# Keys of branch B: the copy in the other half of the partitions made by a DMA, not from PSUM

## The chip, the cores and the metric

The kernel runs on one core of a Trainium2 chip. The metric is device time in microseconds (us) of one execution, as the median of several. Its engines: TensorE (PE in the profile, with its weight loads as PEld), VectorE (DVE), ScalarE (ACT), GpSimd (POOL) and SyncE (SP). DMAs are issued by SP and ACT, each with a hardware queue of its own, called q1 and q10 in the profile.

## The reference

One layer of an encoder with two token mixers in parallel, applied to two inputs apart, a prompt of 1024 tokens and a sample of 512, all in float32, with D_MODEL = 1024:

```
xn = RMSNorm(x)
z  = xn @ W_in            # q_A k_A v_A | q_B k_B v_B | gate_A gate_B
o_A = grouped-query attention, normalised and rotated q/k, 8 heads of 64
o_B = 2-D neighbourhood attention, 8 heads of 64: the tokens are a grid 64 wide;
      each query sees a window of min(8, rows) x 16 tokens, with a learned bias
      by the 2-D offset
mix = (sigmoid(gate_A) * (o_A @ W_pA) + sigmoid(gate_B) * (o_B @ W_pB)) @ W_out
x = x + mix;  x = x + relu(RMSNorm(x) @ W_up)^2 @ W_down;  final RMSNorm
```

The change is in branch B, in how its keys are laid down for the scores `q @ k`.

## The kernel before

**Precision.** A float32 value is kept as two float32r numbers, a high part (a rounded copy) and a low part (the value less its high part). A product of two such values takes three matmuls, high by high, high by low and low by high: the helper `mm3`, whose three matmuls are lines 191, 192 and 193. Splitting costs an ACT copy for the high part and a DVE subtraction for the low part.

**Stages.** The two trunks run one after the other, the sample first, through the function `run`; then the MLP for all tokens. Within `run`, branch B (phase phB) is a stage of its own: from about 181 to 345 us of the span for the sample (T = 512, NB = 1 block of 512 tokens), from about 770 to 1050 us for the prompt (T = 1024, NB = 2).

**Branch B.** Heads go in four pairs (pr = 0 to 3). `qkproj` projects a pair's queries and keys for each block tb of 512 tokens. Each of the two takes 24 matmuls (8 slices of the model dimension, three matmuls each) into one bank of PSUM, tiles `pqbs` and `pkbs`, and is then split into SBUF. The scores of a head contract over 128 partitions where a head has only 64 dimensions: the queries' tile `qBs` has the high part in one half of the partitions and the low part in the other, and the keys' tile `kBs` (one per head, e = 0 or 1) has the same key values in both halves, with the high parts in its plane 0 and the low parts in plane 1. Two matmuls (line 949) then give all the products of parts. Head e of a pair comes out of the projection in the 64 partitions from 64e on, so one half of `kBs` is in place and the other is a copy into the other partitions. Before, both are made from PSUM: two ACT copies (line 909) and two DVE subtractions (line 911) for each head, each of 64 partitions x 512, and eight operations for a block. There are 4 + 8 = 12 blocks, so each of the two lines runs 48 times. The subtractions of either half read the high part of the half that is in place.

The unit of the attention is a head and one or two of the four column strips: `s_unit` makes the scores `sbs` (line 949), the masked and negated scores with their minimum (`sbss`, `msbs`, line 951 on DVE), the exponential `pbs` on ACT (955) and the scaling on POOL (959); `t_unit` transposes the probabilities by TensorE into `ptbs` (974 for the sample, 980 for the prompt) and splits them into `bhs` on ACT (983) and DVE (984); `v_unit` multiplies by the values `vss` into `obs` (1006) and adds the halves up into `os_Bs` (1011 on ACT, 1013 on DVE, 1026 on POOL), which ACT stores (1028, or for the last pair's heads into `oXs`).

**What fills the gaps.** The loop over units (from line 1054 on) runs three units at different stages at once, with the projection of the next pair (`qkproj` is a generator that is advanced eight steps at a time) and with "fill": the projections of gate_B (`gpss`, weights `w_gs`, tanh into `sgs` at line 430, stored as `zgs` by an ACT DMA at 431), and toward the end the projection `ppas` of branch A's output `oXs`, split by line 180 on ACT and 186 on DVE as the weights are.

**What sets the order.** The code gives a program order; the framework then schedules the instructions of all engines by a model of their costs and writes a fixed sequence for each engine. An engine works through its sequence in order. A change to some operations therefore moves others too, on all engines. DMAs that ACT issues stand in ACT's sequence: the issue waits, there, until its data are ready. PSUM has four banks for tiles of 512 columns, shared by `pqbs`, `pkbs`, `gpss`, `ptbs`, `obs` and `ppas`.

Of the kernel before, what the change touches and what calls it, by code (L numbers as in the profile page):

```python
# [11 lines left out]
F32 = mybir.dt.float32  # L12
# [49 lines left out]
def encoder(ctx: ExitStack, tc: tile.TileContext, xs, outs, w):  # L62
    nc = tc.nc
# [23 lines left out]
    def slot(shape, dt, name, left=False):  # L87
        return (s8l if left else s8r).tile(shape, dt, tag="s8", name=name)
# [4 lines left out]
    def mm(name):  # L93
        return pmm.tile([P, 512], F32, tag="mm", name=name)

    def big(name):
        return pbig.tile([P, 1024], F32, tag="big", name=name)
# [92 lines left out]
    def mm3(out, ah, al, bh, bl, start, stop, **kw):  # L190
        nc.tensor.matmul(out, ah, bh, start=start, stop=False, **kw)  # L191
        nc.tensor.matmul(out, ah, bl, start=False, stop=False, **kw)  # L192
        nc.tensor.matmul(out, al, bh, start=False, stop=stop, **kw)  # L193
# [159 lines left out]
    class Trunk:  # L353
# [37 lines left out]
        def xh(self, tb, c):  # L391
            return self.xhl[tb][0][c // 4][:, c % 4, :]

        def xl(self, tb, c):
            return self.xhl[tb][1][c // 4][:, c % 4, :]

    def run(tr, nxt, first):
        N, x, T, NT, NB = tr.N, tr.x, tr.T, tr.NT, tr.NB
# [85 lines left out]
        for g in range(2):  # L484
            with phase(f"phR{N}_{g}") as ph:
# [74 lines left out]
                kT = slot([P, 2, T], F32R, f"kT{N}_{g}")  # L560
# [47 lines left out]
                for tt in range(NT):  # L608
                    tb, j = divmod(tt, 4)
# [233 lines left out]
        with phase(f"phB{N}") as ph:  # L843
# [24 lines left out]
            def qkproj(pr, wqk, dest):  # L868
                wq, wk = wqk
                qT = slot([P, 2, T], F32R, f"qB{N}_{pr}")  # L870
                kT = [slot([P, 2, T], F32R, f"kB{N}_{pr}_{e}") for e in range(2)]
                dest[pr] = (qT, kT)
                for tb in range(NB):
                    cs = slice(tb * 512, tb * 512 + 512)
                    pq = mm(f"pqb{N}_{pr}_{tb}")
                    for k in range(NC8):
                        mm3(pq, wq[k][0], wq[k][1], xh(tb, k), xl(tb, k), k == 0, k == NC8 - 1)
                        yield
                    for e in range(2):
                        hs = slice(64 * e, 64 * e + 64)  # L880
                        ls = slice(64 - 64 * e, 128 - 64 * e)

                        src = pq[hs].rearrange("p (r j c) -> p j r c", j=4, c=16)

                        def strip_view(s_):
                            return qT[s_, e, :].rearrange("p (j r c) -> p j r c", j=4, c=16)[
                                :, :, tb * 8 : tb * 8 + 8, :
                            ]

                        dst_h, dst_l = strip_view(hs), strip_view(ls)  # L890
                        nc.scalar.activation(dst_h, src, AF.Copy, scale=0.125)
                        for jj in range(4):
                            nc.vector.scalar_tensor_tensor(
                                dst_l[:, jj],
                                src[:, jj],
                                0.125,
                                dst_h[:, jj].bitcast(F32),
                                op0=ALU.mult,
                                op1=ALU.subtract,
                            )  # L900
                    pk = mm(f"pkb{N}_{pr}_{tb}")
                    for k in range(NC8):
                        mm3(pk, wk[k][0], wk[k][1], xh(tb, k), xl(tb, k), k == 0, k == NC8 - 1)
                        yield
                    for e in range(2):
                        hs = slice(64 * e, 64 * e + 64)
                        ls = slice(64 - 64 * e, 128 - 64 * e)
                        for os_ in (hs, ls):
                            nc.scalar.activation(kT[e][os_, 0, cs], pk[hs], AF.Copy)
                        for os_ in (hs, ls):  # L910
                            nc.vector.tensor_tensor(
                                kT[e][os_, 1, cs], pk[hs], kT[e][hs, 0, cs].bitcast(F32), op=ALU.subtract
                            )

            qk = {}
# [129 lines left out]
            for _ in qkproj(0, wqk, qk):  # L1045
                pass
# [7 lines left out]
            for i in range(n + LS + LV):  # L1054
# [4 lines left out]
                if i < n:  # L1059
                    s_unit(units[i])  # L1060
                    if units[i][1][0] == 1 and units[i][0] + 1 < 8:
                        prep(units[i][0] + 1)
                    if i % per == (6 if JN == 1 else 2) and i + 2 < n:
                        while held:
                            held.pop(0)()
                        qp = qkproj(i // per + 1, wqk, qk)
                        for _ in range(NC8):
                            next(qp)
                    if i % per == per - 1 and qp is not None:
                        for _ in qp:  # L1070
                            pass
                        qp = None
# [23 lines left out]
        with phase(f"phG{N}") as ph:  # L1096
# [69 lines left out]
            for half in range(2):  # L1166
                wo = wos[half]
                hc = slice(half * 512, half * 512 + 512)
                for tt in range(NT):
                    tb, j = divmod(tt, 4)  # L1170
# [23 lines left out]
                    if half == 0 and NB == 1:  # L1194
                        if tt == 0:
                            both = [big(f"op{N}_{i}") for i in range(2)]
# [36 lines left out]
                    if half == 1:  # L1233
# [5 lines left out]
                        if nxt is None:  # L1239
# [10 lines left out]
                            if 3 <= tt <= 5:  # L1250
# [6 lines left out]
                                both = [big(f"pt0_{j}_{i}") for i in range(2)]  # L1257
# [618 lines left out]
```

## Time and profile before

| | us |
|---|---|
| median of 3 runs | 2132.78 |
| the runs | 2132.7, 2132.78, 2134.22 |
| the profiled execution | 2134.04 |
| its span | 2132.2 |
| sample's branch B, 181 to 345 us | 164.0 |
| prompt's branch B, 770 to 1050 us | 280.0 |

The profile shows one execution. Its span is the time from the first to the last instruction on the core. How its rows are read: a row of the timeline has the start in us, the duration in us, the engine, the line, the operation, output <- inputs by the tiles' names without their numbers, the shape, the number of operations that the row holds, and in brackets how long the engine stood idle before and what released it. A row of waits has the engine, the tile and line that waited, after "<-" what it waited for, then the total in us, the number of times and the longest. A row of windows has start and end, the length, then for each engine the busy time and the number of operations in brackets, TensorE's granted clock (1.00 is full speed), the busy share of the DMA engines and GB/s. A row of a line has how often it ran and the shortest, median and longest duration in ns.

### The profile page before, as it was taken

The page shows a single profiled execution, that of the slowest core. Times are in us where ns is not written, and L with a number is a line of the kernel's source. Part 1 is how long each engine was busy: PE and PEld are TensorE (multiplying, and loading weights), DVE is VectorE, ACT ScalarE, POOL GpSimd, SP SyncE. Part 2 cuts the span into 40 slices and gives each one's busy share as a digit, 9 for nine tenths or more (in the row PEclk, how much of TensorE's full clock was granted, in tenths as well). Part 3 has the DMA queues.
Part 4 walks back from the last instruction along what each step waited for, and adds up shares of the span by engine and source line. Part 5 has one row for each costly group of instructions (what it writes and reads, how often), then busy time and mean ns, then how long its engine had stood idle before and what let it go on. Part 6 is the DMA issues. An engine that isn't in the chain of part 4 may idle for free. (4 is left out here: it accounts for less than half of the span.)

```text
span 2132.2 us, 31826 instructions
## 1 busy us (share of the span) xinstructions
PE 2114.7 (99%) x10982; PEld 1849.5 (87%) x10982; DVE 1473.7 (69%) x2805; ACT 1114.3 (52%) x2345; POOL 388.2 (18%) x506
## 2 busy tenths in 40 slices
PE   9999999999999999999999999999999999999998
PEld 8888788988898888888888999999999988888887
DVE  6675686777667754656782977778777777759563
ACT  5654664556536644655531566566655643434352
POOL 2232420433233223433300200003000000000000
PEclk9999999999999999999999999999999999999999
DMA  6435567620221132433472666578445799688561
GB/s 187 130 105 171 156 187 242 195 72 30 62 83 53 43 108 85 123 106 108 138 247 101 212 200 193 161 249 210 158 145 159 255 351 341 220 275 281 172 197 70
DMA packets 319578, 350.91 MB, mean 165 GB/s; under 512 B 31160, under 2 KB 255032, under 8 KB 319417
## 3 DMA queue, kind: packets, MB, share of 16 engines
q1 hardware_dynamic: 278071, 279.91, 41.8%
q10 hardware_dynamic: 35666, 51.93, 7.0%
q0 software_dynamic: 5680, 17.04, 2.8%
q8 instruction: 87, 1.43, 0.3%
q14 instruction: 74, 0.61, 0.1%
HBM read 264.85 MB, written 87.88 MB: 165 GB/s over the span
## 5 line engine op out<-in xcount | busy, mean ns | idle before, releaser
L193 PE MATMUL dn<-wd,al 128*128 128x512 f32 (+1 forms) x624 | 242.4, 389 | 0.0
L192 PE MATMUL dn<-wd,ah 128*128 128x512 f32 (+1 forms) x624 | 242.4, 388 | 0.0
L191 PE MATMUL dn<-wd,ah 128*128 128x512 f32 (+1 forms) x624 | 242.4, 388 | 0.0
L1289 ACT ACTIVATE ah<-ar 128x512 fp32r<-128x512 f32 x168 | 104.4, 627 | 203.9 <-PE dn L192 183.3
L1290 DVE TENSOR_TENSOR al<-ar,ah 128x512 fp32r<-128x512 f32 x168 | 115.3, 693 | 77.5 <-ACT ah L1289 65.0
L193 PEld LDWEIGHTS dn<-wd,al 128*128 128x128 f32 x624 | 117.2, 188 | 24.2
L192 PEld LDWEIGHTS dn<-wd,ah 128*128 128x128 f32 x624 | 117.2, 188 | 24.1
L191 PEld LDWEIGHTS dn<-wd,ah 128*128 128x128 f32 x624 | 117.2, 188 | 24.0
L735 POOL TENSOR_SCALAR ps<-ps,rls 128x1024 f32<-128x1024 f32 (+1 forms) x96 | 96.8, 1010 | 215.7 <-DVE rls L734 201.3
L775 DVE TENSOR_TENSOR ptls<-pTs,pths 128x512 fp32r<-128x512 f32 x160 | 107.6, 686 | 37.8 <-ACT pths L774 37.1
L774 ACT ACTIVATE pths<-pTs 128x512 fp32r<-128x512 f32 x160 | 94.1, 598 | 73.7 <-PE pTs L769 71.7
L729 DVE TENSOR_REDUCE nms<-ss 128x1 f32<-128x1024 f32 (+1 forms) x96 | 99.8, 1041 | 24.9 <-PE ss L727 24.4
L176 POOL TENSOR_TENSOR rs_f<-ms_f,mhalf 128x1 f32<-128x1 f32 x6 | 4.0, 666 | 590.7 <-DVE ms_f L172 590.7
L732 ACT ACTIVATE ps<-ss,nms 128x1024 f32<-128x1024 f32 (+1 forms) x96 | 93.2, 972 | 23.8 <-DVE nms L729 19.8
L191 PE MATMUL gpss<-xs_0h,w_gs 128*128 128x512 f32 x256 | 104.7, 409 | 0.3 <-ACT w_gs L180 0.2
L769 PEld LDWEIGHTS pTs<-ident,ps 128*128 128x128 f32 x640 | 78.1, 140 | 28.2 <-POOL ps L735 4.1
L193 PE MATMUL gpss<-xs_0h,w_gs 128*128 128x512 f32 x256 | 101.0, 394 | 0.0
L192 PE MATMUL gpss<-xs_0l,w_gs 128*128 128x512 f32 x256 | 100.8, 394 | 0.0
L769 PE MATMUL pTs<-ident,ps 128*128 128x128 f32 x640 | 98.9, 274 | 1.2 <-DVE ptls L775 0.5
L1289 ACT ACTIVATE A<-S 128x512 fp32r<-128x512 f32 x128 | 76.0, 624 | 30.0 <-DVE S L1352 26.8
L1408 ACT ACTIVATE c<-c 128x384 f32<-128x384 f32 x97 | 50.8, 524 | 69.0 <-DVE c L1407 69.0
L1290 DVE TENSOR_TENSOR A<-S,A 128x512 fp32r<-128x512 f32 x128 | 84.4, 685 | 3.4 <-ACT A L1289 3.4
(344 smaller groups left out, 6402.3 us busy)
## 6 DMA issues: line engine op xcount, KB each, us to landing
ar<-ud SPq DMA_DIRECT2D x120, 512.0 KB
br<-in_w_mlp_down_dram SPq DMA_DIRECT2D x72, 512.0 KB
rawu<-in_w_mlp_up_dram SPq DMA_DIRECT2D x64, 512.0 KB
ud<-c ACTq DMA_DIRECT2D x128, 192.0 KB
raw_gs<-in_w_in_dram SPq DMA_DIRECT2D x32, 512.0 KB
zgs<-sgs ACTq DMA_DIRECT2D x48, 256.0 KB
ud<-cs SPq DMA_DIRECT2D x64, 192.0 KB
raw_os<-in_w_out_dram SPq DMA_DIRECT2D x16, 512.0 KB
```

What stands on the lines that cost most here:

```text
L191: nc.tensor.matmul(out, ah, bh, start=start, stop=False, **kw)
L192: nc.tensor.matmul(out, ah, bl, start=False, stop=False, **kw)
L193: nc.tensor.matmul(out, al, bh, start=False, stop=stop, **kw)
L729: nc.vector.tensor_reduce(nm_, s, axis=AX.X, op=ALU.max, negate=True)
L732: nc.scalar.activation(p, s, AF.Exp, bias=nm_, accum_out=l)
L735: nc.gpsimd.tensor_scalar(p, p, rl, 1.0, op0=ALU.mult, op1=ALU.mult)
L769: nc.tensor.transpose(pt[:, j * P : (j + 1) * P], PP[u, j][:, kc * P : (kc + 1) * P], ident)
L774: nc.scalar.activation(hi, pt, AF.Copy)
L775: nc.vector.tensor_tensor(lo, pt, hi.bitcast(F32), op=ALU.subtract)
L1289: nc.scalar.activation(hi, src, AF.Copy)
L1290: nc.vector.tensor_tensor(lo, src, hi.bitcast(F32), op=ALU.subtract)
L1408: nc.scalar.activation(t, t, AF.Relu)
```

## The change

```
-                    for e in range(2):
-                        hs = slice(64 * e, 64 * e + 64)
-                        ls = slice(64 - 64 * e, 128 - 64 * e)
-                        for os_ in (hs, ls):
+                    both = (slice(0, 64), slice(64, 128))
+                    by_dma = pr > 0 or tb + 1 < NB
+                    for e, hs in enumerate(both):
+                        for os_ in (hs,) if by_dma else (hs, both[1 - e]):
                             nc.scalar.activation(kT[e][os_, 0, cs], pk[hs], AF.Copy)
-                        for os_ in (hs, ls):
+                    for e, hs in enumerate(both):
+                        for os_ in (hs,) if by_dma else (hs, both[1 - e]):
                             nc.vector.tensor_tensor(
                                 kT[e][os_, 1, cs], pk[hs], kT[e][hs, 0, cs].bitcast(F32), op=ALU.subtract
                             )
+                    for e, hs in enumerate(both):
+                        if by_dma:
+                            nc.scalar.dma_start(
+                                kT[e][both[1 - e], :, cs].bitcast(F32), kT[e][hs, :, cs].bitcast(F32)
+                            )
```

In 10 of the 12 blocks only the half that is in place is made from PSUM, by one ACT copy and one subtraction for each head. ACT then issues a DMA for each head, which copies high and low part of that half into the other half of the partitions, 256 KB. Two blocks stay as they were: those whose scores follow the first projection, the sample's pair 0 and the second block of the prompt's pair 0. For all twelve, the code now gives both heads' ACT copies, then both heads' subtractions, where it gave one head after the other. In the changed file ACT's copies keep line 909, the subtractions become line 912, the DMAs are line 917, and the lines behind grow by 6 (949 becomes 955, 983 becomes 989, 1006 becomes 1012).

The order of all engines moves with it, inside the two stretches of branch B only. Two places, both at the last pair of the prompt, second block (pair 3; heads 6 and 7; `kBs_3_0` and `kBs_3_1` are the keys of its two heads, the last number of a name is a running number). First ACT's sequence before:

```order
L909 ACTIVATE kBs_3_0_10994<-pkbs_3_1_11146 64x512 x2
L180 ACTIVATE oXs_0_3_11227<-rawos_0_3_11225 128x1024
L983 ACTIVATE bhs_5_0_11188<-ptbs_5_0_0_11189 128x3x128
L983 ACTIVATE bhs_5_0_11188<-ptbs_5_0_1_11190 128x3x128
L909 ACTIVATE kBs_3_1_10995<-pkbs_3_1_11146 64x512 x2
L430 ACTIVATE sgs_3328_7_1_11231<-gpss_3328_7_1_10933 128x512
```

And after, at the same place:

```order
L909 ACTIVATE kBs_3_0_10978<-pkbs_3_1_11128 64x512
L909 ACTIVATE kBs_3_1_10979<-pkbs_3_1_11128 64x512
L180 ACTIVATE oXs_0_3_11207<-rawos_0_3_11205 128x1024
L917 DMA kBs_3_0_10978<-kBs_3_0_10978 64x2x512
L917 DMA kBs_3_1_10979<-kBs_3_1_10979 64x2x512
L989 ACTIVATE bhs_5_0_11168<-ptbs_5_0_0_11169 128x3x128
L989 ACTIVATE bhs_5_0_11168<-ptbs_5_0_1_11170 128x3x128
L430 ACTIVATE sgs_3328_7_1_11211<-gpss_3328_7_1_10917 128x512
```

The second head's copy has moved up beside the first head's, and the two DMAs stand ahead of the copies of `bhs`, which now come behind the DMAs' waits for the subtractions on DVE.

TensorE's sequence at the same place, before; `sbs_6` are the first scores of head 6, `obs_5_2` a unit of head 5:

```order
L193 MATMUL gpss_3328_7_1_10933<-xs_1h_4661,w_gs_3328_7_10636 128x512
L949 MATMUL sbs_6_1_11245<-kBs_3_0_10994,qBs_3_10993 128x384 x2
L949 MATMUL sbs_6_2_11337<-kBs_3_0_10994,qBs_3_10993 128x384 x2
L1006 MATMUL obs_5_2_11234<-bhs_5_2_11021,vss_5_10547 128x512 x2
L1006 MATMUL obs_5_2_11234<-bhs_5_2_11021,vss_5_10547 128x2x128 x2
```

And after:

```order
L193 MATMUL gpss_3328_7_1_10917<-xs_1h_4655,w_gs_3328_7_10620 128x512
L1012 MATMUL obs_5_2_11214<-bhs_5_2_11005,vss_5_10531 128x512 x2
L1012 MATMUL obs_5_2_11214<-bhs_5_2_11005,vss_5_10531 128x2x128 x2
L955 MATMUL sbs_6_1_11225<-kBs_3_0_10978,qBs_3_10977 128x384 x2
L955 MATMUL sbs_6_2_11317<-kBs_3_0_10978,qBs_3_10977 128x384 x2
```

The four matmuls of `obs` have moved ahead of the scores. In the same way 5 gate matmuls have moved ahead of the first scores at the sample's pair 1, 6 gate matmuls and a transpose at its pair 2, and 4 transposes at its pair 3; in the prompt 4 matmuls of `obs` and 2 of the gate at pair 1, and 12 gate matmuls at pair 2.

## The prediction

> **What bounds the kernel now.** I read the head of the page, then the stretch of each trunk in which branch B runs (the only places where the order of instructions changes), cut out by windows, then TensorE's waits in those two stretches.
>
> ```profile
> span 2132.2 us, 31826 instructions
> PE 2114.7 (99%) x10982; PEld 1849.5 (87%) x10982; DVE 1473.7 (69%) x2805; ACT 1114.3 (52%) x2345; POOL 388.2 (18%) x506
> ```
>
> ```profile
> core 0: us, PE busy (x) PEld busy (x) DVE busy (x) ACT busy (x) POOL busy (x), PEclk, DMA share, GB/s
> 181.00:345.00 164.00, 162.07 (x786) 131.75 (x786) 119.60 (x286) 91.44 (x179) 48.09 (x68) 1.00 0.60 187
> 770.00:1050.00 280.00, 277.42 (x1347) 228.20 (x1345) 174.27 (x454) 151.14 (x317) 104.46 (x141) 1.00 0.38 114
> ```
>
> TensorE is busy for 99% of the span. In the sample's stretch (181 to 345 us) it stands idle for 164.00 - 162.07 = 1.93 us, in the prompt's (770 to 1050) for 280.00 - 277.42 = 2.58 us: 4.51 us together, 0.21% of the time. The granted clock is 1.00 in both. The change takes no matmul away, so 4.5 us is all that it can win, whatever it saves on ScalarE (ACT) and VectorE (DVE). What ended those idle times, prompt first, then sample:
>
> ```profile
> PE ptbs L980 <- POOL pbs L959: 0.7, 1, 0.7
> PE gpss L191 <- DVE bhs L984: 0.4, 1, 0.4
> PE obs L1006 <- DVE bhs L984: 0.4, 1, 0.4
> PE sbs L949 <- DVE msbs L951: 0.4, 1, 0.4
> PE ppas L191 <- ACT w_pas L180: 0.3, 1, 0.3
> PE ppas L191 <- DVE kBs L911: 0.2, 1, 0.2
> ```
>
> ```profile
> PE sbs L949 <- DVE msbs L951: 0.9, 3, 0.4
> PE ppas L191 <- ACT sgs L430: 0.7, 1, 0.7
> PE gpss L191 <- ACT w_gs L180: 0.2, 1, 0.2
> ```
>
> The key copies (L909 and L911) release TensorE late in one single row, for 0.2 us. None of these waits is for a DMA.
>
> **What is removed.** The two lines that the change thins out, by their rows:
>
> ```profile
> L909 ACT ACTIVATE kBs<-pkbs x48: 588/592/598, 181.5 to 995.7; 64x512 fp32r<-64x512 f32 x48
> L911 DVE TENSOR_TENSOR kBs<-pkbs,kBs x48: 672/689/696, 182.7 to 997.0; 64x512 fp32r<-64x512 f32 x48
> ```
>
> There are 12 blocks of keys (sample: four head pairs of one block; prompt: four of two), each with four copies on either engine. Ten blocks go by DMA (not the sample's pair 0, and not the second block of the prompt's pair 0), so 20 of the 48 go on each: 20 x 0.592 = 11.8 us from ACT and 20 x 0.689 = 13.8 us from DVE. In the two stretches ACT is busy for 91.44 of 164 and 151.14 of 280 us, DVE for 119.60 and 174.27; neither is the bound, so this pays only where TensorE waits for one of them.
>
> The regrouping also ends the turns that the two engines take on a bank of PSUM. The block of the sample's pair 1, in the timeline:
>
> ```profile
> 210.01 1.19 ACT L909 ACTIVATE kBs<-pkbs 64x512 fp32r<-64x512 f32 x2 [2.40 <-PE pkbs L193]
> 211.24 1.38 DVE L911 TENSOR_TENSOR kBs<-pkbs,kBs 64x512 fp32r<-64x512 f32 x2 [3.43 <-ACT kBs L909]
> 212.65 1.20 ACT L909 ACTIVATE kBs<-pkbs 64x512 fp32r<-64x512 f32 x2 [0.24 <-DVE kBs L911]
> 213.88 1.40 DVE L911 TENSOR_TENSOR kBs<-pkbs,kBs 64x512 fp32r<-64x512 f32 x2 [0.54 <-ACT kBs L909]
> ```
>
> Before, the bank is held from 210.01 to 213.88 + 1.40 = 215.28, 5.27 us. After, one pair of copies on each engine does it: 210.01 to about 211.24 + 1.38 = 212.62. The bank comes free some 2.6 us earlier, and so do the two engines.
>
> Where that can pay: the waits on bhs (0.4 + 0.4), on sgs (0.7), on w_gs (0.2) and on the key copy itself (0.2), all of which stand behind key copies on ACT or DVE. That is 1.9 us, if all of them go. The waits on msbs, pbs and w_pas (0.4 + 0.9 + 0.7 + 0.3) hang on the softmax chain and a late weight, which the change does not shorten; I leave them. **Term 1: -1.9 us.**
>
> **What is added.** Twenty DMAs of 64 partitions x 4 KB = 256 KB, issued by ACT, each from the finished half of a head's tile into its other half. The trace has no transfer of this kind, within SBUF; the nearest is the gate's store of the same size by the same queue:
>
> ```profile
> 798.04 0.33 ACTq L431 DMA_DIRECT2D zgs<-sgs  x1
> ```
>
> ```profile
> GB/s 0 0 0 0 0 0 0 0 0 0 0 0 0 0 0 0 0 287 164 451 451 246 573 246 410 492 246 492 287 451 287 123 41 0 0 0 0 0 0 0
> q10 hardware_dynamic: 144, 0.26, 34.7%
> ```
>
> The second view is the DMA traffic from 798 to 800 us in slices of 0.05 us, all of it ACT's queue (q10). It runs in slices 17 to 32, that is until 799.65: 1.6 us after the issue, of which 0.8 us is traffic. I take 1.66 us from issue to use. The other end is a transfer that met the loads of SyncE's queue (q1); the rows are its issue, the traffic from 206.3 to 209.9, and that from 206.3 to 211.3:
>
> ```profile
> 206.31 0.66 ACTq L1028 DMA_DIRECT2D obds<-os_Bs  x1
> ```
>
> ```profile
> q1 hardware_dynamic: 1841, 0.93, 93.3%
> ```
>
> ```profile
> q1 hardware_dynamic: 2203, 1.39, 93.9%
> q10 hardware_dynamic: 144, 0.07, 5.2%
> ```
>
> In the first 3.6 us ACT's queue moved nothing (no row of q10), and its 64 KB then took until about 211.2: 4.9 us. So a landing costs between 1.66 and 4.9 us, and the lower end, with the same size on the same queue, is the nearer.
>
> The issue itself takes ACT's sequencer 0.33 us, 6.6 us for twenty; it runs beside an operation that ACT has already begun (the two stretches leave ACT 72.6 and 128.9 us idle). The DMAs wait for the low part on DVE, and what stands behind them on ACT waits with them: a copy of bhs or a gate's tanh, until the low part of the second head is done, at most one DVE operation, 0.69 us. I put that at nothing, because ACT has just been spared two copies of 0.592 us at the same place; the price if that cover fails is in the third rival.
>
> **Who waits for the landing.** Scores (sbs, L949) of the pair's first head need its DMA. For a block that is not the pair's last, over 10 us of other matmuls lie between, since the second block's projection alone is 48 matmuls. Six blocks are followed at once by scores: pairs 1, 2 and 3 of the sample, and of the prompt. Their first ACT copies and their first score matmuls, before:
>
> ```profile
> 241.56 1.19 ACT L909 ACTIVATE kBs<-pkbs 64x512 fp32r<-64x512 f32 x2 [2.68 <-PE pkbs L193]
> 273.25 0.59 ACT L909 ACTIVATE kBs<-pkbs 64x512 fp32r<-64x512 f32 x1 [0.96 <-PE pkbs L193]
> 853.77 1.19 ACT L909 ACTIVATE kBs<-pkbs 64x512 fp32r<-64x512 f32 x2 [1.58 <-PE pkbs L193]
> 924.62 1.19 ACT L909 ACTIVATE kBs<-pkbs 64x512 fp32r<-64x512 f32 x2 [1.58 <-PE pkbs L193]
> 992.03 1.19 ACT L909 ACTIVATE kBs<-pkbs 64x512 fp32r<-64x512 f32 x2 [2.49 <-PE pkbs L193]
> ```
>
> ```profile
> 214.16 0.52 PE L949 MATMUL sbs<-kBs,qBs 128*128 128x256 f32 x3
> 245.72 0.41 PE L949 MATMUL sbs<-kBs,qBs 128*128 128x256 f32 x2
> 277.40 0.40 PE L949 MATMUL sbs<-kBs,qBs 128*128 128x256 f32 x2
> 858.33 0.52 PE L949 MATMUL sbs<-kBs,qBs 128*128 128x384 f32 x2
> 927.13 0.95 PE L949 MATMUL sbs<-kBs,qBs 128*128 128x384 f32 x4
> 994.31 1.18 PE L949 MATMUL sbs<-kBs,qBs 128*128 128x384 f32 x4
> ```
>
> From the first ACT copy to the landing: 1.19 (the pair of copies) + 0.69 (low part) + 1.66 + about 0.06 in gaps = 3.6 us. The new order of TensorE puts other matmuls ahead of the scores: 5 of the gate at the sample's pair 1, 6 and a transpose at pair 2, four transposes at pair 3; in the prompt 6, 12 and 4. A matmul takes 277.42 / 1347 = 0.206 us by the window's row, a transpose (a quarter as wide) I count as 0.1. Landing against TensorE's arrival:
>
> - sample pair 1: 213.61 against 214.16 + 1.03 = 215.19, 1.6 us to spare
> - pair 2: 245.16 against 245.72 + 1.34 = 247.06, 1.9
> - pair 3: 276.85 against 277.40 + 0.4 = 277.80, 0.95
> - prompt pair 1: 857.37 against 858.33 + 1.24 = 859.57, 2.2
> - pair 2: 928.22 against 927.13 + 2.47 = 929.60, 1.4
> - pair 3: 995.63 against 994.31 + 0.82 = 995.13, late by 0.5
>
> **Term 2: +0.5 us**, at the last place alone. Its lower bound is nothing. The sum is -1.9 + 0.5 = -1.4 us: the profiled execution's 2134.04 would become 2132.6. That one lies 1.26 us above the median of the three runs, 2132.78, so I forecast 2131.4 for a median.
>
> The gate's store moves at 250 to 570 GB/s in the slices above, by all 128 partitions. [...] No run here shows a transfer between partition halves yet; the sum above goes by the row. [...]
>
> **The rivals.**
>
> *The landing is late at all six places (slower).* Place: the first scores after a pair's last block. Price: if the transfers take 4.9 us, as the one that met SyncE's loads, each lands 3.24 us later than I reckoned, and the waits are 1.7 + 1.3 + 2.3 + 1.0 + 1.9 + 3.7 = 11.9 us, net +10.0: 2142.8. For it: the DMA share is 0.60 in the sample's stretch, and 5.2 MB more are put into the two. Against: the share is 0.38 in the prompt's, and the store at 798 us landed in 1.6 us. It shows as slower once the waits pass 4.27 + 1.9 = 6.2 us, that is from a mean landing of about 3.9 us on. Chance 0.10.
>
> *All idle time goes (faster).* The msbs and pbs waits vanish as well because DVE has 13.8 us less to do: -4.5, 2128.3. For it: msbs comes from DVE. Against: a new order makes its own waits, and no order leaves none. Chance 0.05.
>
> *ACT is held (about +2).* The second DMA's wait for the low part delays what is behind it by up to 0.69 us at each of the six places: at most 4.1 - 1.9 + 0.5 = +2.7, 2135.5. Against: the spared copies. Chance 0.13.
>
> *Waits only change places.* TensorE's new order brings as many small gaps as it removes: 0, 2132.8. For it: the nine rows are single events of under 1 us that any order rearranges. Chance 0.22, with the case that the change does not do what it says, which the orders shown with it speak against (28 copies on each engine are left, and 20 DMAs stand on ACT).
>
> **How the numbers follow.** My forecast has a chance of 0.50. A change within 0.2%, 4.27 us, is about what a measurement of this kernel can't tell from none. Forecast, held ACT and changed places lie within it: 0.50 + 0.13 + 0.22 = 0.85. Slower by more is the late landing, 0.10; faster by more is the loss of all idle time, 0.05. The range leaves out these last two: up to 2135.5 for the held ACT and 0.5 for the spread of runs (2132.7 to 2134.22) makes 2136.0; down, term 1 alone with half of the remaining idle time gone, -1.9 - 1.3 = -3.2, and 0.6 for the spread makes 2129.0.
>
> **What would show it.** ACT's row of L909 with 28 in place of 48, DVE's likewise; banks of keys held for some 2.6 us; the rows of TensorE's waits on sgs, bhs and kBs gone; a wait of the scores for a DMA of 0.3 to 1 us near 995 us and none at the other five; the two windows with TensorE idle for 2 to 5 us together. I am wrong if the scores wait for DMAs at several places, if the DMAs land over 3 us after their issue, or if the idle time of the two windows grows by more than 4 us.

## The result and the profile after

| | before | after |
|---|---|---|
| median of 22 runs each, us | 2132.97 | 2136.97 |
| lowest to highest | 2132.43 to 2134.84 | 2134.58 to 2139.81 |
| profiled execution / its span | 2134.04 / 2132.2 | 2136.61 / 2134.8 |

The change makes the kernel slower by 4.0 us between the medians; the measured ratio is 1.0017, with a 95% interval of 1.0012 to 1.0023. That is just under the 0.2% up to which the prediction spoke of no change, but it is a loss clear of the noise, where a gain of 1.4 us was forecast, and it lies 1 us above the range. The runs also spread twice as far as before, 5.2 us against 2.4.

The stage in which it is lost follows from two matmuls that stand at its start and behind its end: the first of the queries' projection (`pqbs`) and the first of branch B's output projection (`ppbs`). The sample's pair and then the prompt's, in the timeline of before:

```profile
170.40 0.39 PE L191 MATMUL pqbs<-xs_0h,w_bqs 128*128 128x512 f32 x1
308.74 0.39 PE L191 MATMUL ppbs<-oXs,w_pbs 128*128 128x512 f32 x1
767.44 0.39 PE L191 MATMUL pqbs<-xs_0h,w_bqs 128*128 128x512 f32 x1
1060.49 0.40 PE L191 MATMUL ppbs<-oXs,w_pbs 128*128 128x512 f32 x1
```

and of after:

```profile
170.32 0.39 PE L191 MATMUL pqbs<-xs_0h,w_bqs 128*128 128x512 f32 x1
309.18 0.39 PE L191 MATMUL ppbs<-oXs,w_pbs 128*128 128x512 f32 x1
766.45 0.39 PE L191 MATMUL pqbs<-xs_0h,w_bqs 128*128 128x512 f32 x1
1062.84 0.40 PE L191 MATMUL ppbs<-oXs,w_pbs 128*128 128x512 f32 x1
```

The sample's stage went from 138.34 to 138.86 us (+0.5), the prompt's from 293.05 to 296.39 (+3.3). Between the two stages, where the orders are the same, the profiled execution of after was 1.4 us faster. Over the fourteen profiles of this case that stretch takes from 457.3 to 459.2 us, so this is chance, and it is why the two profiles differ by 2.6 us only.

The stages can be cut into pieces, at the first matmul of the key projection (`pkbs`) of each next pair. In every kernel the profile has the same number of matmuls in a piece. The first piece of the prompt ends, before and then after, at

```profile
834.42 0.50 PE L191 MATMUL pkbs<-xs_0h,w_bks 128*128 128x512 f32 x1
834.55 0.50 PE L191 MATMUL pkbs<-xs_0h,w_bks 128*128 128x512 f32 x1
```

It took 834.42 - 767.44 = 66.98 us and 834.55 - 766.45 = 68.10. So 1.1 us of the loss is there, at pair 0. The four pieces of the sample changed by +0.45, +0.39, -0.65 and +0.31 us, those of the prompt by +1.12, 0.01, -0.41 and +2.62.

The lines that answer to those of before. ACT's key copies, now 28 as the change says:

```profile
L909 ACT ACTIVATE kBs<-pkbs x28: 578/592/595, 181.4 to 992.4; 64x512 fp32r<-64x512 f32 x28
```

TensorE's waits in the prompt's stage (770 to 1055 us), then in the sample's (181 to 348):

```profile
PE sbs L955 <- DMA kBs<-kBs: 2.0, 1, 2.0
PE ptbs L986 <- POOL pbs L965: 1.0, 1, 1.0
PE sbs L955 <- DVE msbs L957: 0.4, 1, 0.4
PE obs L1012 <- DVE bhs L990: 0.3, 1, 0.3
PE obs L1012 <- PE gpss L193: 0.3, 1, 0.3
```

```profile
PE sbs L955 <- DMA kBs<-kBs: 0.8, 1, 0.8
PE ptbs L980 <- POOL pbs L965: 0.7, 1, 0.7
PE pqbs L193 <- DVE w_bqs L186: 0.6, 1, 0.6
PE sbs L955 <- DVE msbs L957: 0.3, 1, 0.3
PE ppas L191 <- ACT w_pas L180: 0.3, 1, 0.3
```

The waits on sgs, w_gs and the key copies are gone, as expected, and of those on bhs 0.3 us are left. In their place the scores wait twice for a key DMA, at pair 3 of either trunk, and the sample has new waits on pbs, w_bqs and w_pas. The prompt's pair 3 in the timeline of after (ACT, DVE, ACT's queue, ACT, then TensorE; in brackets the idle time and what ended it):

```profile
991.76 1.21 ACT L909 ACTIVATE kBs<-pkbs 64x512 fp32r<-64x512 f32 x2 [2.33 <-PE pkbs L193]
993.00 1.41 DVE L912 TENSOR_TENSOR kBs<-pkbs,kBs 64x512 fp32r<-64x512 f32 x2 [1.56 <-ACT kBs L909]
993.72 1.41 ACTq L917 DMA_DIRECT2D kBs<-kBs  x2
995.18 0.87 ACT L989 ACTIVATE bhs<-ptbs 128x384 fp32r<-128x384 f32 x2 [1.12 <-DVE kBs L912]
...
997.49 0.95 PE L955 MATMUL sbs<-kBs,qBs 128*128 128x384 f32 x4 [2.05 <-DMA kBs<-kBs]
```

The first head's DMA is issued at 993.72, about as reckoned (993.97, in before's time), and the scores go 3.77 us later, not 1.66. And the stall does not end with the wait. Rows of windows around it (start and end, length, busy time of PE, PEld, DVE, ACT and POOL, granted clock, DMA share, GB/s):

```profile
995.00:997.50 2.50, 0.45 (x4) 0.24 (x3) 1.76 (x4) 1.96 (x4) 0.00 (x0) 1.00 1.01 246
998.50:998.77 0.27, 0.27 (x5) 0.27 (x4) 0.27 (x3) 0.00 (x0) 0.00 (x0) 1.00 1.22 296
998.77:1002.18 3.41, 3.41 (x11) 2.92 (x10) 1.89 (x9) 1.87 (x6) 1.16 (x2) 0.50 1.16 313
1002.50:1010.00 7.50, 7.50 (x39) 6.30 (x38) 5.51 (x14) 4.21 (x11) 4.06 (x6) 1.00 0.27 81
```

From 1.3 us behind the wait TensorE is granted half of its clock, for 3.41 us; 11 operations fit where the next row has 39 in 7.5 us, 18 in 3.41. So 0.5 x 3.41 = 1.7 us are lost to the clock. Wait and clock together make 3.75 us at this one place. The whole piece grew by 2.62: before had waits of its own here, and they went.

Why the landing is late shows where key DMAs run with no other queue in the way. First the two of the prompt's first block: their issue, and the traffic from 780.6 to 783.2 us in slices of 0.065 us:

```profile
779.47 1.41 ACTq L917 DMA_DIRECT2D kBs<-kBs  x2
```

```profile
GB/s 0 0 95 158 252 284 126 252 252 95 347 158 284 126 126 315 158 126 221 158 158 158 189 284 252 410 284 378 284 315 410 315 441 221 284 158 1 0 0 0
q10 hardware_dynamic: 288, 0.52, 79.3%
```

ACT's queue (q10) alone moves here, 0.52 MB in the slices 2 to 35, 34 x 0.065 = 2.2 us: 237 GB/s, against 0.26 MB in 0.8 us, 330 GB/s, of the gate's store before. Traffic begins at 780.73, 1.26 us after the first issue (0.85 for the store), and an issue takes 0.64 us of ACT here and not 0.33. The next view is a key DMA with nothing beside it, in a run told below (x8), from 784.1 to 787.1 us in slices of 0.075 us:

```profile
784.12 0.66 ACTq L915 DMA_DIRECT2D kBs<-kBs  x1
```

```profile
GB/s 0 0 0 0 0 0 0 0 0 0 0 0 0 0 0 0 0 109 164 191 300 137 300 109 300 137 300 137 300 137 273 164 218 164 28 28 0 0 0 0
q10 hardware_dynamic: 144, 0.26, 39.3%
```

It runs in the slices 17 to 35, from 785.4 to 786.8: 0.26 MB in 1.4 us, some 185 GB/s, and done 2.7 us after its issue. One key DMA is slow by itself. The second head's transfer hardly adds to that, for the two go one behind the other. A DMA of this size is 144 packets, 128 large ones and 16 small ones at its end. At the pair above, of the packets from 779.4 to 782.3 us,

```profile
DMA packets 174, 0.32 MB, mean 112 GB/s; under 512 B 16, under 2 KB 16, under 8 KB 174
```

the first head's 16 small ones are already among them, 2.8 us after its issue. And at the prompt's pair 3, where SyncE's queue has traffic too, the queue had moved the first head's 0.26 MB by 996.5, as the row of 995.0 to 996.5 us shows:

```profile
q10 hardware_dynamic: 140, 0.26, 78.1%
```

That is again 2.8 us after the issue, and the scores start 1.0 us later still, at 997.49. So three parts make the 3.77 us: a later first packet (1.3 us and not 0.85), slower traffic (1.4 to 1.5 us and not 0.8), and up to 1.0 us from the traffic to the use, which the prediction's 1.66 us did not contain.

The lone transfer makes 185 GB/s; the two heads' transfers, which write opposite halves, make 237 together.

### The profile page after: what moved, and what is told of

Same layout as the page of the kernel before. It is cut to its first block, busy times and chain, and to the rows that moved or that the text cites. A ratio compares the mean times of both kernels' runs of the same rounds, so it can differ in the third digit from the quotient of the medians.

```text
span 2134.8 us, 31824 instructions
## 1 busy us (share of the span) xinstructions
PE 2115.3 (99%) x10982; PEld 1851.7 (87%) x10982; DVE 1458.4 (68%) x2785; ACT 1104.4 (52%) x2325; POOL 387.0 (18%) x506
## 4 chain that ended last, share of the span: by engine, by line
PE 93%; DVE 2%; DMA 2%; issue 1%; ACT 1%; POOL 1%; SPq 0%; ACTq 0%; POOLq 0%; DVEq 0%
PE dn L193 7%; PE dn L191 7%; PE dn L192 7%; PE gpss L191 4%; PE gpss L193 4%; PE gpss L192 4%; PE pTs L769 3%; PE ud L192 2%; PE uc L192 2%; PE ud L193 2%; PE uc L193 2%; PE uc L191 2%; PE ud L191 2%; PE ua L192 2%; PE ua L193 2%; PE ua L191 2%
```

## The experiments

Theory L (landing): the loss comes from the scores' waits for key DMAs and the reduced clock behind them. Rivals: S, the regrouping of the code and the new sequences make it; I, the DMA issues hold up ACT. All runs were timed against before on their own chip.

**x1_regroup.** No DMA at all, only the new grouping:

```
-                    by_dma = pr > 0 or tb + 1 < NB
+                    by_dma = False
```

> All copies are made from PSUM as before, only the code order is the new one (both heads' ACT copies, then both heads' subtractions); no DMA. Theory L (late landings: in the changed kernel's profile the scores wait for key DMAs for 0.8 us near 279 us and 2.0 us near 997 us, and behind the second wait the granted clock is at 0.55 for some 3.5 us, about 1.6 us more): no landing, so no loss, within 1.5 us of before. Theory S (the regrouping and the new sequences that come with it make the loss): +3 to +5 us against before, as the changed kernel. Theory I (20 DMA issues of about 0.64 us hold ACT up): no issue, within 1 us of before.

Measured: 2139.47 against 2133.37, +6.1 us, ratio 1.0029 (1.0018 to 1.004). L as the only cause has fallen: the regrouping by itself loses more than the whole change. The mechanism shows in the timeline of the prompt's pair 0, first of before:

```profile
778.52 1.19 ACT L909 ACTIVATE kBs<-pkbs 64x512 fp32r<-64x512 f32 x2 [3.31 <-PE pkbs L193]
779.74 1.38 DVE L911 TENSOR_TENSOR kBs<-pkbs,kBs 64x512 fp32r<-64x512 f32 x2 [3.58 <-ACT kBs L909]
781.16 1.20 ACT L909 ACTIVATE kBs<-pkbs 64x512 fp32r<-64x512 f32 x2 [1.45 <-DVE kBs L911]
```

and of this run:

```profile
779.91 2.42 ACT L909 ACTIVATE kBs<-pkbs 64x512 fp32r<-64x512 f32 x4 [3.31 <-PE pkbs L193]
782.36 2.09 DVE L912 TENSOR_TENSOR kBs<-pkbs,kBs 64x512 fp32r<-64x512 f32 x3 [4.81 <-ACT kBs L909]
```

ACT and DVE take turns on the bank: in the profile of before none of the 48 copies overlaps in time with one of the 48 subtractions. With ACT's four copies in a row, DVE stands idle until 2.45 us after the first began, and the first head is complete after 2.45 + 1.38 = 3.8 us, before after 779.74 + 1.38 - 778.52 = 2.6. Every pair's first scores have 1.2 us less to spare, and the four pieces of the prompt grew by 1.08, 1.18, 0.91 and 1.25 us. In the changed kernel, two of the twelve blocks still have all four copies, and their order is this one.

**x2_slack, x3_second, x4_always.** Still grouped; fewer DMAs or more:

```
x2:  by_dma = tb + 1 < NB
x3:  if by_dma and e == 1:        # at the copies and at the DMA
x4:  by_dma = True
```

> DMAs only in the prompt's first blocks of each pair (8 of the 20), where 48 matmuls or more lie between landing and scores; all other blocks as in the run that only regroups. Theory L: no wait of the scores for a DMA, no reduced clock, within 1.5 us of before. Theory S: +3 to +5 us. Theory I: 8/20 of the loss of 4.0 us, +1.6 us.

> Ten DMAs: only the second head of each pair goes by DMA, the first head's other half is copied from PSUM. The second head's scores come several units behind the first's, so theory L has no wait for a DMA and the time within 1.5 us of before. Theory S: +3 to +5 us. Theory I: half the issues, +2.0 us.

> All twelve blocks go by DMA, 24 of them: also the sample's pair 0 and the prompt's second block of pair 0, whose scores follow the projection at once. Theory L: two more waits, each 2 to 3.7 us long plus up to 1.6 us of reduced clock behind it: +8 to +14 us against before. Theory S: as the changed kernel, +3 to +5 us. Theory I: 24/20 of 4.0, +4.8 us.

Measured: x2 2139.26, +5.9 (1.0016 to 1.0039); x3 2137.69, +4.3 (1.0012 to 1.0029); x4 2137.71, +4.3 (1.001 to 1.0028), all against 2133.37. In x2 eight blocks have the four copies in a row and it loses like x1; x3 has a row of three copies in the ten blocks. I as the only cause has fallen: x1 has no issue, x2 8 of the 20, and both lose more than the changed kernel. x4 missed theory L's number and fits those of S and I: the two blocks whose scores follow at once did not wait. In the sample the scheduler had put gate matmuls ahead of them, so that the first scores come at 186.94 us; before, they came at 182.72:

```profile
186.94 0.41 PE L955 MATMUL sbs<-kBs,qBs 128*128 128x256 f32 x2
```

**x6_turns, x8_turns_second, x9_turns_slack.** Head by head, as before: copy, subtraction, DMA of one head, then the other.

```
for e, hs in enumerate(both):
    by_dma = pr > 0 or tb + 1 < NB                  # x6
    by_dma = e == 1 and (pr > 0 or tb + 1 < NB)     # x8
    by_dma = tb + 1 < NB or e == 1 and pr > 0       # x9
    ... ACT's copies, DVE's subtractions, the DMA
```

> The same 20 DMAs as the changed kernel, but head by head as before: one head's ACT copy, its subtraction, its DMA, then the other head. The two blocks without DMAs have before's order. Theory G (the regrouping makes the loss: in the run that only regroups ACT's four copies stand in a row for 2.42 us and the first subtraction starts only then, so that the first head is ready 3.8 us after the projection and not 2.6; the DMAs win some of it back): the loss goes, and by plain addition of the two parts (+6.1 for the regrouping, +4.0 for the whole) -2 us is left, between -3 and 0. Theory L (the waits for the landings carry a part of their own): the first head's DMA is issued 0.6 us earlier, so the waits of 0.8 and 2.0 us shrink to 0.2 and 1.4 and the reduced clock behind them stays: +1 to +2.5 us.

> Head by head, and only the second head of each of the ten blocks by DMA (10 DMAs); the first head's two halves from PSUM as before. No scores wait for a landing, and the first head is ready as early as before. Theories G and L alike: -1.5 to +0.5 us. If DMA issues on ACT or the mere new sequences cost: +2 us or more.

> Head by head; both heads by DMA in the prompt's first blocks of each pair (far ahead of their scores), only the second head by DMA in the last blocks of pairs 1 to 3, none in pair 0's last blocks: 14 DMAs, none of which scores wait for. Theories G and L alike: -2 to 0 us. If DMA issues or the mere new sequences cost: +2.5 us or more.

Measured against 2133.7: x6 2137.96, +4.3 (1.0012 to 1.003); x8 2135.21, +1.5 (0.9999 to 1.0017); x9 2135.38, +1.7 (1.0 to 1.0018). x6 refutes the addition of the two parts (-2 expected), and is above what L expected too. In the sample's pair 3 its scores wait 1.1 us for a key DMA; its loss at the prompt's pair 3 is of a third kind:

```profile
993.73 0.68 DVE L911 TENSOR_TENSOR kBs<-pkbs,kBs 64x512 fp32r<-64x512 f32 x1 [0.30 <-ACT kBs L909]
994.45 0.65 ACTq L915 DMA_DIRECT2D kBs<-kBs  x1
995.14 0.59 ACT L909 ACTIVATE kBs<-pkbs 64x512 fp32r<-64x512 f32 x1 [0.50 <-issue]
995.76 0.87 ACT L987 ACTIVATE bhs<-ptbs 128x384 fp32r<-128x384 f32 x2
996.80 0.93 PE L1010 MATMUL obs<-bhs,vss 128*128 128x512 f32 x4 [1.24 <-issue]
```

The issue stands in ACT's sequence between the two heads. It waits for the subtraction, takes 0.65 us, and the second head's copy and the copies of bhs come behind it; TensorE has `obs` next in line, not the scores, and waits 1.24 us there. (The label "issue" names no releaser; that it is bhs follows from the order on ACT and the input of `obs`.) x8 and x9, where no scores wait for a landing, miss what L and G expected (-1.5 to +0.5, -2 to 0). Their intervals reach down to no change, but in the profiles the two stages together are 2.3 us longer than before in either. A part of that is waits that before does not have; the longest is in the sample, of x8 here (x9 has it with 1.15 us):

```profile
259.48 0.51 PE L953 MATMUL sbs<-kBs,qBs 128*128 128x256 f32 x2 [1.32 <-DVE msbs L955]
```

Nothing waits for a landing there, and nothing is regrouped. So the new sequences, with the DMAs' issues in them, cost something by themselves, as a part of S has it.

**x7_kept_by_head.** The changed kernel, with before's order in the two blocks without DMAs:

```
+                    for heads in ((0, 1),) if by_dma else ((0,), (1,)):
+                        for e in heads: ...   # ACT's copies
+                        for e in heads: ...   # DVE's subtractions
```

> The changed kernel, with before's head by head order in the two blocks that have no DMA; the ten blocks with DMAs stay grouped. Theory G with its place in the two blocks without DMAs: the profile of the changed kernel loses about 1.3 us against before between the first scores of the prompt's pair 0 and the transposes behind them, so +2.7 us against before. If the grouping costs in the blocks with DMAs alone: +4 us as the changed kernel. If it costs in the two blocks alone: -2 to 0 us.

Measured: 2135.92 against 2133.7, +2.2 us (1.0002 to 1.0019); the number expected was +2.7. The medians differ from the changed kernel's by 1.8 us, but the two intervals overlap. The pieces settle it: the first of either trunk takes 33.71 and 66.98 us, as before, where the changed kernel had 34.16 and 68.10. So 1.6 us of the loss come from the order in two blocks in which no DMA is used. What is left shows as the same waits at pair 3 (2.0 and 0.8 us), and one more at the prompt's pair 1, where the changed kernel's profile had none:

```profile
PE sbs L958 <- DMA kBs<-kBs: 2.8, 2, 2.0
```

**x10_not_last, x12_extra_ahead, x14_one_dma, x15_first_blocks.** The first three are x7 with one edit to pair 3's last block in either trunk, the fourth is x6 with fewer DMAs:

```
x10:  by_dma = 0 < pr < 3 or tb + 1 < NB
x12:  nc.scalar.dma_start(spare, kT[0][both[0], :, cs].bitcast(F32))   # 256 KB to DRAM, ahead of the two
x14:  if by_dma and e not in copied:                      # copied = (1,): second head from PSUM
x15:  by_dma = tb + 1 < NB
```

> As the run that keeps the two blocks without DMAs head by head (+2.2 us against before), and in addition the last block of pair 3 of either trunk is made from PSUM head by head: 16 DMAs are left. Theory L (the landing at pair 3: waits of 0.8 and 2.0 us and about 1.2 us of reduced clock behind the longer one): both waits and the reduced clock are gone, -1.8 to +0.5 us against before. If the mere new sequences of the other blocks make what is left: still +1.5 to +3 us.

> As the run that keeps the two blocks head by head, with one more DMA of 256 KB (the first head's finished half, to a spare place in DRAM) ahead of the first head's DMA in the last block of pair 3 of either trunk. Theory L: the first head lands 1.2 to 1.7 us later, the waits grow from 0.8 to some 2.2 us and from 2.0 to some 3.5 us, each with a reduced clock behind it: +5 to +7 us against before. If the landing is not what costs: +2 us as without the extra DMA.

> As the run that keeps the two blocks head by head, but in the last block of pair 3 of either trunk only the first head goes by DMA; the second head's halves come from PSUM. If the second head's DMA, issued 0.8 us behind, slows the first one's landing: the wait near 997 us falls from 2.0 to 1.2 us or less, no reduced clock, 0 to +1 us against before. If SyncE's loads slow it: the wait stays at 1.6 us or more (four transposes stand ahead of the scores now, 0.4 us), +1.5 to +2.5 us.

> Head by head as before, DMAs only in the prompt's first blocks (8 DMAs), whose scores come over 10 us later; the sample's branch B is as before. Theories G and L: -1 to +0.5 us against before. If each DMA issue on ACT costs by itself: 8/20 of 4.0, +1.6 us.

Measured against 2133.56. x12: 2143.98, +10.4 us (1.0032 to 1.0059), above the +5 to +7 expected. The one more DMA ahead made the waits of the scores, sample and prompt,

```profile
PE sbs L961 <- DMA kBs<-kBs: 3.6, 1, 3.6
```

```profile
PE sbs L961 <- DMA kBs<-kBs: 2.8, 1, 2.8
```

in place of 0.8 and 2.0, and both now have the reduced clock behind them, in the sample for twice as long:

```profile
281.44:288.26 6.82, 6.58 (x20) 5.42 (x21) 2.54 (x10) 2.83 (x7) 2.91 (x5) 0.50 0.54 149
```

There 3.4 us are lost to it, twice what the other places lose. Against x7 the sample's last piece grew by 6.0 us, about the 2.8 of longer wait and the 3.4 of clock.

x10, which takes the DMAs out of the same place: 2135.1, +1.5 us, an interval that holds no change (0.9996 to 1.0015), no wait for a DMA and no reduced clock. The time lies outside what L expected (-1.8 to +0.5) and at the foot of what the new sequences would leave (+1.5 to +3). By the median it is 0.7 less than x7. In the profiles the prompt's last piece is 1.27 us longer than before's, and that of x7 2.83. So taking the landing out of this place gave back 1.6 us, not the 3.7 of wait and clock: the sequence that comes instead has waits of its own, as one of 0.9 us of the transposes on `os_Bs`. That a later landing costs is shown by x12; what this one makes of the 4.0 us is some 1.4 to 1.6, by one profile of each kernel.

x14: 2137.68, +4.1 us (1.001 to 1.0027): a miss on the time for either side. The first head's DMA is alone in its queue here, and its 144 packets are all among those of 995.0 to 998.1 us, 2.95 us after its issue at 995.15:

```profile
995.15 0.64 ACTq L921 DMA_DIRECT2D kBs<-kBs  x1
```

```profile
q10 hardware_dynamic: 144, 0.26, 43.2%
```

That is no earlier than in the changed kernel, where 0.26 MB had gone 2.8 us after the issue. So the second DMA does not slow the first to speak of. Nor do SyncE's loads by much: with no other queue it was 2.7 us. The time went elsewhere. ACT's three copies stand in a row ahead of the subtraction, the DMA's issue behind it, the copies of bhs behind that, and `obs` waits:

```profile
996.65 0.94 PE L1016 MATMUL obs<-bhs,vss 128*128 128x512 f32 x4 [1.61 <-issue]
```

x15: 2133.97, +0.4 us, ratio 1.0 (0.9992 to 1.0009). Eight DMAs with over 10 us ahead of their scores, and the two heads in turns, cost nothing and win nothing, though they take 8 copies off ACT and 8 off DVE. The interval by itself reaches theory I's +1.6, but in the profile none of the eight pieces differs from before by more than 0.03 us, so the issues had no price by themselves. x2 has the same eight DMAs and loses 5.9 us; what sets the two apart is the grouping, with the sequences that come of it.

The pieces of the main kernels, as their differences from before in us, each from one profiled execution:

| | sample, pair 0 | 1 | 2 | 3 | prompt, pair 0 | 1 | 2 | 3 | both stages |
|---|---|---|---|---|---|---|---|---|---|
| changed | +0.45 | +0.39 | -0.65 | +0.31 | +1.12 | +0.01 | -0.41 | +2.62 | +3.9 |
| x1 | +0.46 | +0.95 | -0.05 | +0.94 | +1.08 | +1.18 | +0.91 | +1.25 | +6.7 |
| x7 | 0.00 | +0.42 | -0.69 | +0.23 | 0.00 | +1.04 | -0.41 | +2.83 | +3.4 |
| x10 | +0.01 | +0.36 | -0.69 | +0.95 | +0.04 | +0.08 | -0.41 | +1.27 | +1.6 |
| x12 | +0.05 | +0.36 | -0.74 | +6.21 | +0.05 | +0.04 | -0.41 | +3.93 | +9.5 |
| x15 | -0.01 | -0.01 | -0.03 | -0.01 | 0.00 | -0.03 | -0.01 | -0.03 | -0.1 |

## Why the prediction was wrong

- **Right: the bound, and the count.** TensorE bounds both stages (busy for 136.18 of 138.86 us and 291.87 of 296.39 after), and fewer copies on ACT and DVE pay only where TensorE waits for them: 8 less gained nothing (x15). The cap of 4.5 us on any gain held.
- **Right in kind: where a landing would be felt.** The one place forecast, the prompt's pair 3, is the one with the long wait.
- **Term 2, "+0.5 us", failed in its size.** It priced a landing at 1.66 us by the row nearest in size, the gate's store to DRAM. At pair 3 the key DMA's data could be used 3.77 us after its issue: the first packet at about 1.3 us and not 0.85, 1.4 to 1.5 us of traffic and not 0.8, and up to 1.0 us more from there to the scores, where the 1.66 us ended with the last packet. The row that was nearest in bytes was not nearest in kind: it used 128 partitions, the key DMA 64. Wait at the prompt's pair 3: 2.05 us; at the sample's: 0.8, where 0.95 had been to spare. Two of the signs that the prediction had named came with it, a landing over 3 us after its issue and a second place with a wait.
- **The reduced clock was in no term and no rival.** A wait was priced at its own length. Behind the 2.05 us wait it cost 1.7 us more; x12 raised both waits and showed it at both places.
- **The step "the regrouping also ends the turns" was half read.** It is right for the blocks with DMAs, where a bank is free earlier. The text called the other two blocks unchanged but for the code's order and priced them at nothing; there the turns were what got the first head ready early, at 2.6 and not 3.8 us. x1 shows the price over all twelve blocks, 6.1 us, and x7 that of the two, 1.6 us.
- **Term 1, -1.9 us, came to -1.06 at most.** The waits that it named did go, but for 0.3 us on bhs, and two pieces became shorter, the sample's pair 2 by 0.65 us and the prompt's by 0.41. They did so in x7, x10 and x12 too, and not in x1, which has no DMAs. Waits on pbs, w_bqs and w_pas came at other places, as the rival "waits only change places" had it; the sample's pair 1 lost 0.39.
- **The rival "ACT is held"** is real, but in x6 and x14 (1.24 and 1.61 us at one place), where the issue stands between ACT's copies or behind three of them; in the changed kernel ACT stood idle 1.12 us behind it, and TensorE did not wait for that.

By cause, then, in the profile's 3.9 us: 1.6 from the two kept blocks, 2.6 from the prompt's pair 3 with its late landing and the clock, 0.7 from the sample's pairs 1 and 3, where waits on `w_bqs` and on a key DMA are new, less 1.1 won at the two trunks' pair 2. The first is shown by x7, which took away just that. Of the 2.6, x10 puts 1.4 on the landing and its clock; the other 1.3 stayed with a new sequence, and which of its waits make them is open. No version beat before; the best, x15, is level with it.

## What to carry to other kernels

When a copy is handed to a DMA, ask first who reads it and how soon: from the issue to the use of the copy it was 3.8 us here, and blocks whose readers came over 10 us later bore it for nothing (x15). Price it by a transfer with the same partitions, not only the same bytes (256 KB took 1.4 us of traffic from 64 partitions here, 0.8 from 128), and up to the start of its reader, not up to its last packet. And read a change in pieces that hold the same work: the medians here spread over 2 us and more, while a piece with the same order of TensorE's work, as pair 0 of either trunk in x7, x10 and x15, agreed within 0.05 us. And where two engines share one PSUM bank by turns, "all of one, then all of the other" delays the first result that a waiting engine needs (3.8 us and not 2.6 here, x1), even though the sum of the work is the same.

## What the runs showed of the hardware

- **Behind waits of TensorE of 2.0 us and more its granted clock was 0.50 for 3.4 us or longer.** Behind waits of 2.0 to 2.1 us (the changed kernel, x4, x7) and of 2.8 us (x12, prompt) the granted clock was 0.50 for some 3.4 us (3.41 in the changed kernel), and 1.7 us were lost; behind 3.65 us (x12, sample) it was 0.50 for 6.8 us, and 3.4 were lost. Behind 1.61 us (x14) and 1.24 (x6) there was nothing of the kind. The stretches of one clock have lengths that are multiples of 3.413 us: in the changed kernel the clock was full for 986.45 us ahead of the slow stretch and for 1129.81 behind it, 289 and 331 times that, and before's one full stretch, of 2116.26 us, is 620 times that. With the time cut into steps of this length from the clock's first record on, the slow stretch of the changed kernel follows the step in which TensorE was idle longest, 2.05 us (995.36 to 998.77 us); behind the next longest, 0.97 us (278.56 to 281.97), the clock stayed full, as it did in before, where no step up to TensorE's last matmuls had more than 0.85 us of idle time. Why x12's slow stretch in the sample lasts 6.8 us is not shown.
- **256 KB from 64 partitions landed later than 256 KB from 128.** A key DMA alone was done 2.7 us after its issue, the gate's store after 1.6. The destination does not make it: x12's extra DMA, from 64 partitions to DRAM, moved its 0.26 MB in the 1.2 us from 1001.2 to 1002.4, about as slowly as the copies within SBUF (2.2 us for two, 1.4 for one alone), where the gate's store took 0.8:

```profile
q10 hardware_dynamic: 127, 0.26, 96.8%
```

- **The runs of the changed kernel are less steady**, 5.2 us from lowest to highest against 2.4. DMAs alone do not do it, since x9 with 14 of them spreads over 2.2 us. The same landing showed a wait at the prompt's pair 1 in x7's profile and none in the changed kernel's. What makes the spread is not shown.
